# Splitting one 256-column product in five channel units of each FFN of a decoder trunk

## The chip, the core and the metric

The kernel runs on one core of a Trainium2 chip. The metric is the device time of one execution in microseconds, the median of several runs. The core's engines are TensorE (PE in the profile, with its weight loads shown apart as PEld), VectorE (DVE), ScalarE (ACT), GpSimd (POOL) and SyncE (SP), which issues most transfers.

## What is computed

Two decoder layers over a sequence of 256 tokens with 1024 channels, in fp32. Each layer is a SwiGLU FFN at half weight, a token mixer (a state-space branch and a gated delta-rule branch side by side), and a second FFN. Only the FFN matters here; there are four in all.

```python
def swiglu(x, w_in, w_out):
    gate, up = jnp.split(x @ w_in, 2, axis=-1)
    return (jax.nn.silu(gate) * up) @ w_out

for l in range(DEPTH):
    h = h + 0.5 * swiglu(rms_norm(h, ffn1_norm[l]), ffn1_w_in[l], ffn1_w_out[l])
    ...
    h = h + merged @ w_out[l]
    h = h + 0.5 * swiglu(rms_norm(h, ffn2_norm[l]), ffn2_w_in[l], ffn2_w_out[l])
return rms_norm(h, final_norm)
```

Here `w_in` has 1024 rows and 5632 columns (2816 gates and 2816 ups), and `w_out` 2816 rows and 1024 columns.

## The kernel before

**Precision.** Every large product is done in three matmuls. Each fp32 operand is kept as a rounded part (`whi`, `uTh`) and the remainder (`wlo`, `uTl`), both of a rounded fp32 type that TensorE takes in one pass. The helper `mm3w` (lines 300 to 303) multiplies rounded weights with rounded input, rounded weights with the input's remainder, and the weights' remainder with the rounded input, all into the same PSUM columns. In the profile these are lines L301, L302 and L303. `mm3` (L296 to L298) is the same with the activations as the stationary operand and 512 columns of weights moving.

**Weights.** All weights come through one stream of 512 KB pieces in DRAM. `load` starts a transfer into one of five `wraw` buffers (or a `wfirst` buffer for the first piece of a group), `prep` rounds it on ScalarE into one of five `whi` buffers (L67) and takes the remainder on VectorE into `wlo` (L70). `take` hands the next pair to the matmuls and keeps the preparation up to five pieces ahead. For some pieces VectorE also takes differences of raw weights (the `wfirst<-wraw,wfirst` and `wraw<-wraw` rows).

**One FFN.** The string `FFN` gives its order. First come 256 gate and up columns by tokens (`f`, tile `f`). Then follow 20 *channel units* (`c`, tile `fc`), each 128 gate and 128 up columns: `chan_chunk` takes two weight pieces and runs, for gate and for up (`a`), over eight blocks `kt` of 128 input channels, one `mm3w` each. This makes 48 matmuls of 256 columns (the 256 tokens), each with a weight load of 128 by 128. Behind a unit ScalarE takes the silu of the gate half (`sg`) and VectorE multiplies with the up half (`g2`). Four transposes (tile `gT`, L498) stand between the first and the second unit.

The output product `w_out` is done partly in blocks in which seven products of sums and differences stand for eight, as in Strassen's scheme (`block_sums` on the activations, differences in `prep` on the weights). Its first four products of each block pair are the *groups* (`A`, tile `p`, 24 matmuls of 512 columns each), and they stand between channel units: behind the first 8 units, then behind 4, 4 and 2 more. The last 2 units follow the fourth group. Then the *last stage* (`B` and `d`, tile `o`) does the remaining block products and the plain ones, while VectorE adds up the blocks in `join` (tiles `u`, `h`).

**Order.** The program text sets the order on TensorE. On the other engines a scheduler places the instructions by its own estimate of when each can run; the pools (five `whi`, five `wlo`, five `wraw`, four `acc` banks in PSUM) set when a buffer may be written again.

Of the kernel before, what the change touches and what calls it, by code (L numbers as in the profile page):

```python
# [16 lines left out]
P = 128  # L17
# [19 lines left out]
FFN = "f" + 8 * "c" + "A" + 4 * "c" + "A" + 4 * "c" + "A" + 2 * "c" + "A" + 2 * "c" + "BdBBBddddd"  # L37
# [15 lines left out]
def trunk_kernel(ctx, tc, x, wst, wsm, norms, lpar, rpar, cst, out):  # L53
    nc = tc.nc
    V, A, G, PE = nc.vector, nc.scalar, nc.gpsimd, nc.tensor
# [10 lines left out]
    def act(o, i, func=AF.Copy, **kw):  # L66
        return A.activation(out=o, in_=i, func=func, **kw)  # L67

    def tt(o, a, b, op):
        return V.tensor_tensor(out=o, in0=a, in1=b, op=op)  # L70
# [9 lines left out]
    def f(ap):  # L80
        return ap.bitcast(F32)

    def tmp2(name):
        return s2.tile([P, 512], F32, tag="s2", name=name)
# [97 lines left out]
    def take():  # L182
        j = state["taken"]
        state["taken"] = j + 1
        ahead("loaded", min(plan[min(j + NSPL, n_forms) - 1][2] + NRAW - 1, n_raw), load)
        ahead("prepped", min(j + 1 if state["hold"] else j + NSPL, n_forms), prep)
        return halves.pop(j)
# [109 lines left out]
        PE.matmul(ps, lh, rl, start=False, stop=False)  # L297
        return PE.matmul(ps, ll, rh, start=False, stop=stop)  # L298

    def mm3w(ps, wh, wl, mh, ml, start, stop):  # L300
        PE.matmul(ps, wh, mh, start=start, stop=False)  # L301
        PE.matmul(ps, wh, ml, start=False, stop=False)  # L302
        PE.matmul(ps, wl, mh, start=False, stop=stop)  # L303

    def tok_chunk(ps, ks):
# [13 lines left out]
                        kt == KT - 1,  # L319
                    )  # L320

    def chan_chunk(ps):

        ws = [take(), take()]
        for a in range(2):
            for q in range(2):
                wh, wl = ws[q]
                for k in range(4):
                    kt = 4 * q + k
                    c0 = k * 256 + a * P  # L330
                    mm3w(
                        ps[:, a * 256 : (a + 1) * 256],
                        wh[:, c0 : c0 + P],
                        wl[:, c0 : c0 + P],
                        uTh[:, kt, :],
                        uTl[:, kt, :],
                        kt == 0,
                        kt == KT - 1,
                    )

    def out_chunks(ps, stat, ks, last, group=1, split=False, first=None):
# [87 lines left out]
    def ffn(nxt):  # L429
        gh = [slots.tile([P, 8, S], F32R, tag=t_, name="gh") for t_ in ("sA", "sB", "sC")]  # L430
        gl = [slots.tile([P, 8, S], F32R, tag=t_, name="gl") for t_ in ("sD", "sE", "sF")]

        bsa = slots.tile([P, 2, 2, 3, P], F32R, tag="sG", name="bsa")
        bsb = slots.tile([P, 16, P], F32R, tag="sH", name="bsb")
        bsc = slots.tile([P, 4, 2, P], F32R, tag="sI", name="bsc")
        bsd = s2.tile([P, 2, 2, P], F32R, tag="s2", name="bsd")
        bsb3 = bsb[:, 0:12].rearrange("p (i o j) t -> p i o j t", i=2, o=2)
        bsb1 = bsb[:, 12:16].rearrange("p (i o) t -> p i o t", i=2)

        def sums(p, j):  # L440

            q, i = (p - 1) // 2, (p - 1) % 2
            if j < 3:
                b = (bsa[:], bsb3)[q % 2]
                return b[:, i, 0, j, :], b[:, i, 1, j, :]
            b = (bsc[:, 0:2], bsc[:, 2:4], bsb1, bsd[:])[q]
            return b[:, i, 0, :], b[:, i, 1, :]

        def block_sums(p, g2):

            sf = tmp2("sf")
            a11, a21, a12, a22 = (g2[:, j * P : (j + 1) * P] for j in range(4))
            s1, s2_, s3, s4 = (sf[:, j * P : (j + 1) * P] for j in range(4))
            tt(s1, a21, a22, ALU.add)
            tt(s3, a11, a21, ALU.subtract)
            tt(s2_, s1, a11, ALU.subtract)
            tt(s4, a12, s2_, ALU.subtract)
            q, i = (p - 1) // 2, (p - 1) % 2
            h3, l3 = ((bsa[:], bsb3)[q % 2][:, i, o] for o in range(2))
            h1, l1 = sums(p, 3)  # L460
            s3v = sf[:, 0 : 3 * P].rearrange("p (j t) -> p j t", j=3)
            act(h3, s3v)
            act(h1, s4)
            tt(l3, s3v, f(h3), ALU.subtract)
            tt(l1, s4, f(h1), ALU.subtract)

        def split(k0, bv):
            oh = gh[k0 // 8][:, k0 % 8 : k0 % 8 + 2, :]
            ol = gl[k0 // 8][:, k0 % 8 : k0 % 8 + 2, :]
            act(oh, bv)  # L470
            tt(ol, bv, f(oh), ALU.subtract)

        def stat(k, t):
            return (gh[k // 8][:, k % 8, t * P : (t + 1) * P], gl[k // 8][:, k % 8, t * P : (t + 1) * P])

        ps = [accb("f0"), accb("f1")]
        tok_chunk(ps, range(KT))
        gt = []
        for t in range(2):
            sg = tmp2("sg")  # L480
            act(sg[:, 0:256], ps[t][:, 0:256], AF.Silu)
            tt(sg[:, 256:512], sg[:, 0:256], ps[t][:, 256:512], ALU.mult)
            gt.append(sg[:, 256:512])
        todo, pb, n = FFN[1:], {}, 0
        for c in range(FC - 1):
            g2 = tmp2("g2")
            for a in range(2):
                ps = accb("fc")
                chan_chunk(ps)
                sg = s2.tile([P, S], F32, tag="ca", name="sg", bufs=2)  # L490
                act(sg[:], ps[:, 0:S], AF.Silu)
                tt(g2[:, a * S : (a + 1) * S], sg[:], ps[:, S : 2 * S], ALU.mult)
                todo = todo[1:]
                if c == 0 and a == 0:
                    bank = trb("gT")
                    for k in range(2):
                        for t in range(2):
                            PE.transpose(bank[:, k * S + t * P : k * S + (t + 1) * P], gt[t][:, k * P : (k + 1) * P], ident)  # L498
                    split(0, bank[:].rearrange("p (k t) -> p k t", k=2))
            split(2 * c + 2, g2[:].rearrange("p (k t) -> p k t", k=2))  # L500
            if c + 1 <= PAIRS[-1][-1]:
                block_sums(c + 1, g2)
            if todo[0] == "A":
                if not pb:
                    pb.update({i: trb(f"p{i}") for i in (1, 6, 5, 7)})
                four = [
                    (pb[1], lambda p: stat(2 * p, 0), PAIRS[n]),
                    (pb[5], lambda p: sums(p, 0), PAIRS[n]),
                    (pb[7], lambda p: sums(p, 2), PAIRS[n]),
                    (pb[6], lambda p: sums(p, 1), PAIRS[n]),  # L510
                ]
                block_products(four, n == 0, n == len(PAIRS) - 1)
                todo = todo[1:]
                n += 1
        po = [[accb("o"), accb("o")] for _ in range(2)]

        return close_blocks(po, stat, sums, pb, nxt)
# [841 lines left out]
```

## Time and profile before

| | us |
|---|---|
| median of three runs | 1576.33 |
| lowest and highest of them | 1573.42, 1577.17 |
| the profiled execution | 1574.73 |
| its span, first to last instruction | 1573.0 |
| first FFN, first channel unit to last stage | 25.12 to 160.25 |
| groups of output products in the first FFN, start | 70.60, 98.70, 126.75, 143.50 |
| channel units of the other FFNs, start | 618.05, 804.08, 1393.89 |

The granted TensorE clock of the profiled execution has a mean of 0.999 of full speed. A row of a group has the line, the engine, the operation, the output tile and the inputs, the shapes and the count; then the busy time, the mean length of one instruction, and the idle time before them. Matmuls are pipelined: a 256-column matmul is shown some 0.28 us long, while the next one starts 0.11 to 0.12 us later. How fast a stream runs is therefore read from start to start, not from lengths. A timeline row gives start and length in us, and in square brackets how long its engine had been idle and what ended that.

### The profile page before, as it was taken

The numbers are of one execution on the slowest core, as the hardware profiler recorded it, in microseconds if no ns is written. First come the engines' busy times: TensorE is split into PE (matmuls) and PEld (weight loads), VectorE is DVE, ScalarE is ACT, GpSimd is POOL, SyncE is SP. The second block draws the span as 40 slices with busy tenths as digits, with TensorE's granted clock in tenths as the row PEclk, the third lists the DMA queues.
The fourth block names the chain that finished last, engine by engine and source line by source line (L and its number), as shares of the span: only waits on it lengthen the run. The fifth ranks groups of instructions, "written<-read, shape, count | busy, mean of one in ns | idle before, by whom it ended". The sixth has DMA issues, their size and how long they took to land.

```text
span 1573.0 us, 28904 instructions
## 1 busy us (share of the span) xinstructions
PE 1544.0 (98%) x11432; PEld 1393.4 (89%) x11432; DVE 1254.2 (80%) x1888; ACT 950.7 (60%) x1534; POOL 53.8 (3%) x60
## 2 busy tenths in 40 slices
PE   8999999999999999999999999999999999999997
PEld 7999779999888888999789997899998888899995
DVE  6878868967899766878777888699589987677887
ACT  5656568766666645555555566776756665455554
POOL 0000010000000000000000001010000000000000
PEclk9999999999999999999999999999999999999999
DMA  8565565553565566565765456555345556555554
GB/s 297 199 201 186 185 213 188 168 164 114 180 212 164 183 205 192 169 207 181 243 206 191 166 186 223 192 188 188 115 137 200 175 185 215 176 191 187 161 186 133
DMA packets 94221, 293.12 MB, mean 186 GB/s; under 512 B 22325, under 2 KB 23301, under 8 KB 93062
## 3 DMA queue, kind: packets, MB, share of 16 engines
q1 hardware_dynamic: 94086, 291.29, 56.5%
q8 instruction: 89, 1.46, 0.4%
q14 instruction: 46, 0.38, 0.1%
HBM read 289.33 MB, written 1.92 MB: 185 GB/s over the span
## 4 chain that ended last, share of the span: by engine, by line
PE 68%; DVE 14%; DMA 7%; issue 5%; ACT 4%; POOL 1%; SPq 0%; POOLq 0%; ACTq 0%; DVEq 0%
PE fc L301 9%; PE fc L302 9%; PE fc L303 9%; DVE wlo L70 7%; DMA wraw<-in_wst_dram 4%; PE b L298 3%; PE t L297 3%; PE t L296 2%; PE t L298 2%; PE b L297 2%; PE b L296 2%; DVE ca L73 2%; ACT whi L67 2%; PE p L297 2%; PE p L298 2%
## 5 line engine op out<-in xcount | busy, mean ns | idle before, releaser
L70 DVE TENSOR_TENSOR wlo<-wraw,whi 128x1024 fp32r<-128x1024 f32 x488 | 592.3, 1222 | 176.8 <-ACT whi L67 172.3
L67 ACT ACTIVATE whi<-wraw 128x1024 fp32r<-128x1024 f32 x488 | 511.9, 1060 | 276.9 <-PE fc L302 96.0
L301 PE MATMUL fc<-uW,whi 128*128 128x256 f32 x1280 | 359.2, 281 | 0.0
L303 PE MATMUL fc<-uW,wlo 128*128 128x256 f32 x1280 | 358.9, 280 | 0.0
L302 PE MATMUL fc<-uW,whi 128*128 128x256 f32 x1280 | 358.9, 280 | 0.0
L303 PEld LDWEIGHTS fc<-uW,wlo 128*128 128x128 f32 x1280 | 243.6, 190 | 0.0
L301 PEld LDWEIGHTS fc<-uW,whi 128*128 128x128 f32 x1280 | 241.7, 189 | 0.8
L302 PEld LDWEIGHTS fc<-uW,whi 128*128 128x128 f32 x1280 | 240.3, 188 | 0.8
L67 ACT ACTIVATE whi<-wfirst 128x1024 fp32r<-128x1024 f32 x64 | 68.0, 1062 | 65.9 <-PE fc L302 50.9
L296 PE MATMUL t<-whi,uW 128*128 128x512 f32 x256 | 102.1, 400 | 0.0
L297 PE MATMUL t<-wlo,uW 128*128 128x512 f32 x256 | 100.6, 393 | 0.4 <-DVE wlo L70 0.4
L298 PE MATMUL t<-whi,uW 128*128 128x512 f32 x256 | 100.7, 393 | 0.0
L70 DVE TENSOR_TENSOR wlo<-wfirst,whi 128x1024 fp32r<-128x1024 f32 x64 | 78.3, 1223 | 8.8 <-ACT whi L67 8.8
L296 PE MATMUL b<-whi,bh 128*128 128x512 f32 x192 | 76.3, 399 | 0.3 <-ACT bh L67 0.2
L297 PE MATMUL b<-wlo,bh 128*128 128x512 f32 x192 | 74.9, 390 | 0.0
L298 PE MATMUL b<-whi,bl 128*128 128x512 f32 x192 | 74.3, 394 | 0.6 <-DVE bl L70 0.6
L70 DVE TENSOR_TENSOR wfirst<-wraw,wfirst 128x1024 f32<-128x1024 f32 x48 | 58.7, 1222 | 19.1 <-DMA wraw<-in_wst_dram 18.7
L301 PE MATMUL xs<-uW,whi 128*128 128x256 f32 x256 | 72.7, 284 | 0.0
L297 PE MATMUL o<-wlo,gh 128*128 128x512 f32 x160 | 64.5, 403 | 7.1 <-DVE wlo L70 6.9
L303 PE MATMUL xs<-uW,wlo 128*128 128x256 f32 x256 | 71.1, 278 | 0.0
L302 PE MATMUL xs<-uW,whi 128*128 128x256 f32 x256 | 71.0, 277 | 0.0
L296 PE MATMUL o<-whi,gh 128*128 128x512 f32 x160 | 62.1, 392 | 0.3 <-ACT whi L67 0.3
(315 smaller groups left out, 3385.8 us busy)
## 6 DMA issues: line engine op xcount, KB each, us to landing
wraw<-in_wst_dram SPq DMA_DIRECT2D x504, 512.0 KB, 4.5
wfirst<-in_wst_dram SPq DMA_DIRECT2D x16, 512.0 KB, 6.1
dc<-rdram SPq DMA_DIRECT2D x8, 1024.0 KB, 8.5
nw<-in_norms_dram SPq DMA_DIRECT2D x6, 512.0 KB, 5.9
gb<-rdram SPq DMA_DIRECT2D x8, 256.0 KB, 5.5
h<-in_x_dram SPq DMA_DIRECT2D x4, 256.0 KB, 5.9
out_dram<-fo SPq DMA_DIRECT2D x4, 256.0 KB, 2.0
dq<-X SPq DMA_DIRECT2D x2, 256.0 KB, 5.4
```

Of the source, the lines that this page charges most:

```text
L67: return A.activation(out=o, in_=i, func=func, **kw)
L70: return V.tensor_tensor(out=o, in0=a, in1=b, op=op)
L73: return V.scalar_tensor_tensor(out=o, in0=a, scalar=s, in1=b, op0=op0, op1=op1)
L296: PE.matmul(ps, lh, rh, start=start, stop=False)
L297: PE.matmul(ps, lh, rl, start=False, stop=False)
L298: return PE.matmul(ps, ll, rh, start=False, stop=stop)
L301: PE.matmul(ps, wh, mh, start=start, stop=False)
L302: PE.matmul(ps, wh, ml, start=False, stop=False)
L303: PE.matmul(ps, wl, mh, start=False, stop=stop)
```

## The change

In five channel units of each FFN, one of the 48 matmuls is replaced by two of 128 columns each: first and second half of the tokens, with the same weights, into the two halves of the same PSUM columns. It is the product of rounded weights and the input's remainder, at `a == 0` and `kt == 1`, so the fifth matmul of the unit. The five units are the third one (`c == 1`, `a == 0`) and the first one behind each of the four groups. What is computed stays the same.

```diff
-    def mm3w(ps, wh, wl, mh, ml, start, stop):
+    def mm3w(ps, wh, wl, mh, ml, start, stop, cut=False):
         PE.matmul(ps, wh, mh, start=start, stop=False)
-        PE.matmul(ps, wh, ml, start=False, stop=False)
+        if cut:
+            PE.matmul(ps[:, :P], wh, ml[:, :P], start=False, stop=False)
+            PE.matmul(ps[:, P:], wh, ml[:, P:], start=False, stop=False)
+        else:
+            PE.matmul(ps, wh, ml, start=False, stop=False)
         PE.matmul(ps, wl, mh, start=False, stop=stop)
...
-    def chan_chunk(ps):
+    def chan_chunk(ps, cut=False):
...
                         kt == 0,
                         kt == KT - 1,
+                        cut and a == 0 and kt == 1,
                     )
...
-        todo, pb, n = FFN[1:], {}, 0
+        todo, pb, n, cut = FFN[1:], {}, 0, False
...
-                chan_chunk(ps)
+                chan_chunk(ps, cut or (c, a) == (1, 0))
+                cut = False
...
-                todo = todo[1:]
+                todo, cut = todo[1:], True
                 n += 1
```

On TensorE, at the start of the third unit of the first FFN, the program had these rows (the number behind a tile's name tells buffers of one name apart; L301 to L303 are the three matmuls of one `mm3w`):

```order
L301 MATMUL fc_425<-uW_108,whi_281 128x256 [waits PE_49,Activation_49]
L302 MATMUL fc_425<-uW_108,whi_281 128x256
L303 MATMUL fc_425<-uW_108,wlo_282 128x256 [waits DVE_49]
L301 MATMUL fc_425<-uW_108,whi_281 128x256
L302 MATMUL fc_425<-uW_108,whi_281 128x256
L303 MATMUL fc_425<-uW_108,wlo_282 128x256
```

and now has these (line 303 and 304 are the halves, 306 and 307 the old second and third matmul):

```order
L301 MATMUL fc_425<-uW_108,whi_281 128x256 [waits PE_49,Activation_49]
L306 MATMUL fc_425<-uW_108,whi_281 128x256
L307 MATMUL fc_425<-uW_108,wlo_282 128x256 [waits DVE_49]
L301 MATMUL fc_425<-uW_108,whi_281 128x256
L303 MATMUL fc_425<-uW_108,whi_281 128x128
L304 MATMUL fc_425<-uW_108,whi_281 128x128
L307 MATMUL fc_425<-uW_108,wlo_282 128x256
```

One row has become two, and no wait has come or gone. The same stands behind each group, where the last rows of the group (tile `p6`) run straight into the unit:

```order
L297 MATMUL p6_847<-wlo_781,bsa_177 128x512 [waits DVE_49]
L298 MATMUL p6_847<-whi_780,bsa_177 128x512
L296 MATMUL p6_847<-whi_780,bsa_177 128x512
L297 MATMUL p6_847<-wlo_781,bsa_177 128x512
L298 MATMUL p6_847<-whi_780,bsa_177 128x512
L301 MATMUL fc_899<-uW_108,whi_852 128x256 [waits Activation_49]
L306 MATMUL fc_899<-uW_108,whi_852 128x256
L307 MATMUL fc_899<-uW_108,wlo_853 128x256 [waits DVE_49]
L301 MATMUL fc_899<-uW_108,whi_852 128x256
L303 MATMUL fc_899<-uW_108,whi_852 128x128
L304 MATMUL fc_899<-uW_108,whi_852 128x128
L307 MATMUL fc_899<-uW_108,wlo_853 128x256
```

Before, the row of line 303 and the row of line 304 were one row of line 302 there too. The scheduler, which sees two instructions more, has also moved a few rows on the other engines, the same ones in each FFN. On VectorE, around the preparation of the last group's weights, the order was

```order
L70 TENSOR_TENSOR wlo_1569<-wfirst_1507,whi_1568 128x1024 [waits PE_49,Activation_49]
L70 TENSOR_TENSOR g2_1555<-sg_1621,fc_1556 128x256 [waits Activation_49]
L70 TENSOR_TENSOR wfirst_1507<-wraw_1531,wfirst_1507 128x1024 [waits DVE_49]
L70 TENSOR_TENSOR wlo_1626<-wraw_1519,whi_1625 128x1024 [waits Activation_49]
L70 TENSOR_TENSOR wlo_1631<-wfirst_1507,whi_1630 128x1024 [waits PE_49,Activation_49]
```

and is now

```order
L70 TENSOR_TENSOR wlo_1572<-wfirst_1510,whi_1571 128x1024 [waits PE_49,Activation_49]
L70 TENSOR_TENSOR wlo_1630<-wraw_1522,whi_1629 128x1024 [waits PE_49,Activation_49]
L70 TENSOR_TENSOR g2_1558<-sg_1625,fc_1559 128x256 [waits Activation_49]
L70 TENSOR_TENSOR wfirst_1510<-wraw_1534,wfirst_1510 128x1024 [waits DVE_49]
L70 TENSOR_TENSOR wlo_1635<-wfirst_1510,whi_1634 128x1024 [waits PE_49,Activation_49]
```

The remainder of the group's third piece has gone ahead of a `g2`, and carries a wait for TensorE itself; on ScalarE the rounding of the same piece has gone ahead of the `sg` that `g2` reads. In the last stage VectorE had

```order
L70 TENSOR_TENSOR wlo_1970<-wraw_1871,whi_1969 128x1024 [waits Activation_49]
L70 TENSOR_TENSOR wlo_1980<-wfirst_1507,whi_1979 128x1024 [waits Activation_49]
L73 SCALAR_TENSOR_TENSOR u2_1961<-p7_848,u2_1961 128x512
L70 TENSOR_TENSOR wlo_1992<-wraw_1904,whi_1991 128x1024 [waits DMAHW1_49,Activation_49]
L70 TENSOR_TENSOR wlo_2004<-wraw_1906,whi_2003 128x1024 [waits DMAHW2_49,Activation_49]
```

and now has

```order
L70 TENSOR_TENSOR wlo_1975<-wraw_1876,whi_1974 128x1024 [waits Activation_49]
L73 SCALAR_TENSOR_TENSOR u2_1966<-p7_849,u2_1966 128x512
L70 TENSOR_TENSOR wlo_1985<-wfirst_1510,whi_1984 128x1024 [waits Activation_49]
L70 TENSOR_TENSOR wlo_1997<-wraw_1909,whi_1996 128x1024 [waits DMAHW1_49,Activation_49]
L70 TENSOR_TENSOR wlo_2009<-wraw_1911,whi_2008 128x1024 [waits DMAHW2_49,Activation_49]
```

An addition of `join` has gone ahead of one remainder. Two more remainders change places there with the row next to them, once with a `g2` and once with the next addition, and on SP one weight transfer changes places with its neighbour.

## The prediction

> **What bounds the kernel now.** I read the page first (busy shares, chain of waits, groups), then the stretches of the channel units (busy time, count and clock by window), then single rows of the timeline.
>
> ```profile
> PE 1544.0 (98%) x11432; PEld 1393.4 (89%) x11432; DVE 1254.2 (80%) x1888; ACT 950.7 (60%) x1534; POOL 53.8 (3%) x60
> PE 68%; DVE 14%; DMA 7%; issue 5%; ACT 4%; POOL 1%; SPq 0%; POOLq 0%; ACTq 0%; DVEq 0%
> L302 PE MATMUL fc<-uW,whi 128*128 128x256 f32 x1280 | 358.9, 280 | 0.0
> ACT whi L67 <- PE fc L302: 35.1, 29, 3.1
> ```
>
> TensorE holds 68% of the chain, and its `fc` matmuls (the channel units) wait for nothing: idle time before them is 0.0. The last row is from the waits of ScalarE between 25 and 165 us, most of the first FFN: the engine that prepares the weights waited 35.1 us for TensorE there. So a channel unit takes as long as its 48 matmuls take, and their pace is the price. That pace has two values. The next rows are windows restricted to the `fc` tile on PE (from:to, length, busy and count, granted clock, DMA share, GB/s); the windows from 37, 630, 815 and 1406 us are the same units of FFN one to four.
>
> ```profile
> 37.00:70.00 33.00, 33.00 (x282) 1.00 0.59 202
> 630.00:663.00 33.00, 33.00 (x283) 1.00 0.50 156
> 815.00:848.00 33.00, 33.00 (x294) 1.00 0.50 155
> 1406.00:1439.00 33.00, 33.00 (x282) 1.00 0.49 155
> 105.00:126.00 21.00, 21.00 (x181) 1.00 0.55 180
> ```
>
> The third FFN issues 294 matmuls in 33 us, the others 282 or 283. The clock is 1.00 in all, and the second and fourth have the third's DMA share, so neither clock nor transfers make the difference. Exact starts (start, length, engine and line) at both ends of six whole units:
>
> ```profile
> 36.68 0.28 PE L301 MATMUL fc<-uW,whi 128*128 128x256 f32 x1
> 70.60 0.39 PE L296 MATMUL p<-whi,gh 128*128 128x512 f32 x1
> 815.63 0.28 PE L301 MATMUL fc<-uW,whi 128*128 128x256 f32 x1
> 848.27 0.39 PE L296 MATMUL p<-whi,gh 128*128 128x512 f32 x1
> ```
>
> Slow pace: (70.60 - 36.68) / 288 = 117.8 ns a matmul. Quick pace: (848.27 - 815.63) / 288 = 113.3 ns. The difference, 4.44 ns, is 0.21 us a unit. The windows at 105 us and those like it behind the other groups (x181 in 21 us) show the slow pace in every unit behind a group of output products. What sets it? The handover rows:
>
> ```profile
> 75.86 0.39 PE L298 MATMUL p<-whi,bsa 128*128 128x512 f32 x1
> 76.09 0.28 PE L301 MATMUL fc<-uW,whi 128*128 128x256 f32 x1
> 30.59 0.60 PE L498 MATMUL gT<-cs,sg 128*128 128x128 f32 x4
> 30.95 0.36 PE L301 MATMUL fc<-uW,whi 128*128 128x256 f32 x1
> 31.15 0.28 PE L302 MATMUL fc<-uW,whi 128*128 128x256 f32 x1
> 31.27 0.28 PE L303 MATMUL fc<-uW,wlo 128*128 128x256 f32 x1
> 810.41 0.28 PE L303 MATMUL fc<-uW,wlo 128*128 128x256 f32 x1
> 810.53 0.28 PE L301 MATMUL fc<-uW,whi 128*128 128x256 f32 x1
> 811.10 0.28 PE L303 MATMUL fc<-uW,wlo 128*128 128x256 f32 x1
> ```
>
> The same four transposes stand before the second unit of each FFN: in the first FFN the stream behind them stays slow (31.27 - 31.15 = 0.12 us), in the third it settles at 0.114 us ((811.10 - 810.53) / 5). So the pace is a state of the stream: once entered it holds until something narrower or wider comes between, and the same code can land in either. Groups of 512-wide products always hand over into the slow one.
>
> **The change part by part.** Each cut replaces one 256-wide matmul, the fifth of its unit, by two of 128 columns with a weight load each. There are five a FFN, twenty in all.
>
> *Price of a cut.* The trace has no split of these products. The nearest rows are 128-wide matmuls with loads of their own:
>
> ```profile
> 381.16 1.05 PE L901 MATMUL vnb<-rh,TT 128*128 128x128 f32 x8
> 382.18 0.28 PE L302 MATMUL xs<-uW,whi 128*128 128x256 f32 x1
> L226 PE MATMUL nw<-row,one 1*128 1x512 f32 x4 | 3.7, 1085 | 2.3 <-DMA row<-in_norms_dram 2.3
> ```
>
> Between 381.16 and 382.18 lie eight narrow matmuls and one 256-wide: 1.02 / 9 = 0.113 us each; the transposes give (31.15 - 30.59) / 5 = 0.112. Two halves then cost 2 x 0.112 = 0.224 instead of 0.118: +0.106 us. From below: the columns are the same 256, so with the second load hidden the cut is free, 0; nothing in it can gain by itself. From above: the program issues two `nw` matmuls and the trace has four, so plain fp32 runs twice; if narrow halves ran like that, 4 x 0.112 - 0.118 = +0.33 us. I take 0.106, from the row with the same width and load. The Trainium skill (TensorE: Matmul & The Clock Gate, Back-to-back issue gap) gives about 81 ns for a load and a 128-wide matmul in a stream; by it the cut would cost an estimated 0.044 us, and the forecast be 1 us lower. The rows here, at 112 ns, disagree with it.
>
> *What a cut may bring.* It disturbs the locked stream: two narrow steps, then the 256-wide ones go on. If the stream relocks quick, every matmul behind it until the next group saves 4.44 ns. In the third unit 283 matmuls follow (6 x 48 - 5): 1.26 us. The first, second and fourth FFN are slow there: 3 x 1.26 = 3.77 us. The third is quick already; I take it to stay so, 0. Behind the groups stand 4, 4, 2 and 2 units, so 187, 187, 91 and 91 matmuls follow. The first three make 465 x 4.44 ns = 2.06 us a FFN, 8.26 us in all.
>
> *What the other engines make of it.* Preparation must follow. In the third FFN's quick stretch VectorE, the busier of the two, was busy 29.69 of 38 us:
>
> ```profile
> 810.00:848.00 38.00, 38.00 (x338) 38.00 (x336) 29.69 (x47) 20.97 (x31) 0.00 (x0) 1.00 0.53 166
> 142.22 1.06 ACT L67 ACTIVATE whi<-wfirst 128x1024 fp32r<-128x1024 f32 x1 [2.58 <-PE fc L302]
> 143.31 1.23 DVE L70 TENSOR_TENSOR wlo<-wfirst,whi 128x1024 fp32r<-128x1024 f32 x1 [1.05 <-ACT whi L67]
> 155.82 1.23 DVE L70 TENSOR_TENSOR wfirst<-wraw,wfirst 128x1024 f32<-128x1024 f32 x1 [3.24 <-DMA wraw<-in_wst_dram]
> 165.61 4.73 DMA wraw<-in_wst_dram
> 171.51 2.35 DVE wlo L70 x2
> ```
>
> Up to 143 us VectorE and ScalarE still wait for TensorE (1.05 and 2.58 us), so gains before that come through. From there VectorE's only long pause is for a transfer that its own work releases, and the chain through the last output stage (the last two rows, from the chain of waits) is VectorE and DMA. So I count nothing for the two units behind the fourth group, at 149 to 160 us: they could give 91 x 4.44 ns = 0.40 us less a cut, 0.30 us a FFN, 1.2 us in all. The fourth cut behind a group hides in the same way.
>
> *The moved rows.* ScalarE takes one weight rounding ahead of a `sg`, VectorE the remainder of it ahead of `g2`: same work, same release, and the product that comes later is not read before the last stage. In the last stage VectorE takes an addition of `join` ahead of a remainder:
>
> ```profile
> 176.65 1.22 DVE L70 TENSOR_TENSOR wlo<-wfirst,whi 128x1024 fp32r<-128x1024 f32 x1
> 177.79 0.69 DVE L73 SCALAR_TENSOR_TENSOR u<-p,u 128x512 f32<-128x512 f32 x1
> 178.39 1.22 DVE L70 TENSOR_TENSOR wlo<-wraw,whi 128x1024 fp32r<-128x1024 f32 x1
> 178.51 0.39 PE L297 MATMUL o<-wlo,gh 128*128 128x512 f32 x1
> ```
>
> That remainder, needed at 178.51, would end 0.60 us (178.39 - 177.79) later, at 178.47 instead of 177.87: just in time, so 0; without that cover up to 0.6 us a FFN. The two other swaps there have more room. One weight transfer changes places with its neighbour on SP, free as long as ScalarE's wait for TensorE lasts.
>
> *Sum.* 3.77 + 8.26 = 12.03 us gained; 4 cuts x 4 FFNs x 0.106 = 1.70 us paid: 10.3 us net. The profiled execution took 1574.73 us with a span of 1573.0; so span 1562.7, that execution 1564.4, and on the median of the three runs 1576.33 - 10.3 = 1566.0 us. A measurement here tells about 0.3%, 4.7 us, from no change.
>
> **Rivals.**
>
> 1. *The cut does not change the pace.* For: the transposes, narrow too, left three FFNs of four slow. Against: the third FFN, which left it behind the same rows, and the first unit of the first FFN, which starts slow and turns quick by itself:
>
> ```profile
> 25.36 0.28 PE L303 MATMUL fc<-uW,wlo 128*128 128x256 f32 x1
> 25.47 0.28 PE L301 MATMUL fc<-uW,whi 128*128 128x256 f32 x1
> 29.91 0.28 PE L301 MATMUL fc<-uW,whi 128*128 128x256 f32 x1
> 30.25 0.28 PE L301 MATMUL fc<-uW,whi 128*128 128x256 f32 x1
> ```
>
> (three steps from 29.91 to 30.25 are 113 ns each). Then only the cuts remain: 16 to 20 x 0.106 = 1.7 to 2.1 us, 1578.2. The Trainium skill (same page and section) knows one gap a width, 256 / 2.4 + 2.5 = 109 ns, and no second pace; by that rule a cut could only cost. The two paces of the trace disagree with it.
>
> 2. *It changes at some places.* Only behind the groups: 8.26 - 1.70 = 6.6 us, 1569.8. Only in the third units: 3.77 - 1.70 = 2.1, 1574.3. Or at all of them with dear halves: 12.03 - 16 x 0.33 = 6.8, 1569.6. For it: the two kinds of place come from different streams, transposes and 512-wide products.
>
> 3. *Dear halves with no change of pace, slower.* Place: the two narrow matmuls of each cut. At 0.33 us each, 16 to 20 of them cost 5.3 to 6.6 us: 1582. It decides from 4.7 / 16 = 0.29 us a cut. For: no narrow product of these rounded operands stands in the trace. Against: narrow matmuls run at 0.112 us a pass.
>
> **How the numbers follow.** Forecast 0.47, rival 1 0.20, rival 2 0.20 (0.13 of it over 4.7 us of gain, 0.07 within), rival 3 0.13. Faster 0.47 + 0.13 = 0.60, same 0.20 + 0.07 = 0.27, slower 0.13. The forecast's own range is 1563 to 1569. The low end of the whole: 1566.0 less 1.2 (fourth groups count) less 1.7 (free cuts) less some 1.5 for seven units of the mixer that could relock quick (0.21 each): 1561.5. The high end stops between rivals 1 and 3, at 1580.
>
> **What would show it.** Right: windows at 37, 630 and 1406 us with some 294 `fc` matmuls in 33 us, those behind the groups with about 185 in 21; 0.22 us across the halves; the output stage about 2 us earlier a FFN with no more idle time before its `o` matmuls. Wrong: 282 and 181 again (rival 1); a mix (rival 2); 0.45 us across the halves (rival 3); a quick third FFN turned slow by its cut, which costs 1.26 us; `o` matmuls that wait for VectorE by as much as the units gained.

## The result, and the profile after

| kernel | us, median | lowest to highest | runs |
|---|---|---|---|
| before | 1576.59 | 1573.42 to 1577.17 | 4 |
| changed | 1568.47 | 1566.61 to 1569.1 | 4 |

The ratio is 0.9954, with a 95% interval of 0.9939 to 0.9969 (it is taken over the runs; the quotient of the two medians is 0.9949). By the medians the change takes 8.1 us off, where 10.3 us were forecast. The profiled execution took 1568.61 us with a span of 1566.8, against 1573.0 before, a difference of 6.2 us. In two later sets of runs, each beside the kernel before on one chip, the same kernel gave 1567.93 and 1567.06 us (ratios 0.9965, 0.9952 to 0.9977, and 0.9955, 0.9943 to 0.9967), so 6 to 8 us is the size of it.

The page of the changed kernel, the rows that answer to those shown of before:

```profile
PE 1535.5 (98%) x11452; PEld 1382.9 (88%) x11452; DVE 1252.7 (80%) x1888; ACT 949.7 (61%) x1534; POOL 53.7 (3%) x60
PE 67%; DVE 16%; DMA 6%; issue 5%; ACT 4%; POOL 1%; SPq 1%; POOLq 0%; ACTq 0%; DVEq 0%
L306 PE MATMUL fc<-uW,whi 128*128 128x256 f32 x1260 | 348.1, 276 | 0.0
L297 PE MATMUL o<-wlo,gh 128*128 128x512 f32 x160 | 65.4, 409 | 9.8 <-DVE wlo L70 9.6
```

TensorE still carries the chain, with twenty matmuls more (11452 against 11432) and 8.5 us less busy time; VectorE's share of the chain rose from 14 to 16%. The last row is the price side. On the page of before it reads:

```profile
L297 PE MATMUL o<-wlo,gh 128*128 128x512 f32 x160 | 64.5, 403 | 7.1 <-DVE wlo L70 6.9
```

So the output stages of the changed kernel wait 2.7 us longer for VectorE's remainders (9.6 against 6.9 us, all four FFNs).

The pace is read from windows on the `fc` tile (from:to, length, busy and count, granted clock, DMA share, GB/s). Of the changed kernel, the first behind the third unit's cut and the other two behind the first two groups of the first FFN:

```profile
37.50:68.50 31.00, 31.00 (x276) 1.00 0.62 206
80.00:95.00 15.00, 15.00 (x134) 1.00 0.44 149
108.00:122.00 14.00, 14.00 (x126) 1.00 0.45 152
```

Before, the same window behind the first group:

```profile
80.00:95.00 15.00, 15.00 (x130) 1.00 0.53 178
```

At 113.3 ns a window of 15 us holds 132 starts and at 117.8 ns 127, with up to three more that were under way at its edges; the counts of 134 and 130 are the quick and the slow pace, at the same granted clock. (The windows of 33 us that the prediction named cannot be filled: the 283 matmuls behind the third unit's cut take 32.1 us at the quick pace.) From start to start every one of the twenty cuts has the quick pace behind it; in three of the four third units the stream had been quick ahead of the cut as well. One cut row by row, the first behind a group:

```profile
74.35 0.39 PE L298 MATMUL p<-whi,bsa 128*128 128x512 f32 x1
74.58 0.28 PE L301 MATMUL fc<-uW,whi 128*128 128x256 f32 x1
74.70 0.28 PE L306 MATMUL fc<-uW,whi 128*128 128x256 f32 x1
74.81 0.28 PE L307 MATMUL fc<-uW,wlo 128*128 128x256 f32 x1
74.93 0.28 PE L301 MATMUL fc<-uW,whi 128*128 128x256 f32 x1
75.05 0.22 PE L303 MATMUL fc<-uW,whi 128*128 128x128 f32 x1
75.11 0.28 PE L304 MATMUL fc<-uW,whi 128*128 128x128 f32 x1
75.22 0.33 PE L307 MATMUL fc<-uW,wlo 128*128 128x256 f32 x1
75.39 0.28 PE L301 MATMUL fc<-uW,whi 128*128 128x256 f32 x1
75.51 0.29 PE L306 MATMUL fc<-uW,whi 128*128 128x256 f32 x1
...
75.98 0.28 PE L307 MATMUL fc<-uW,wlo 128*128 128x256 f32 x1
76.09 0.28 PE L301 MATMUL fc<-uW,whi 128*128 128x256 f32 x1
```

The stream arrives at 117 to 118 ns. The first half is over in 0.06 us (75.05 to 75.11), the second takes 0.11, and the matmul behind them 0.17 (75.22 to 75.39). From the first half to 75.39 is 0.345 us by the trace's nanoseconds, where two slow matmuls take 0.236: the cut costs 0.109 us. The weight loads (PEld) in this place start at 75.05, 75.17, 75.28 and 75.40 us, so they stand 0.11 us apart, further than the 0.06 us that the first half took. A few steps later the stream stands at 0.113 and stays there.

Where the time went, by stage. The *channel stage* of an FFN runs from the start of the first `fc` matmul to the start of the first `o` matmul, and the *last stage* from there to the start of the next part's first product (`t` or `f`; for the fourth FFN to the last matmul's end). In the first FFN these two starts are 25.12 and 160.25 us before and 25.00 and 156.83 us after; the second edge of the changed kernel:

```profile
156.72 0.28 PE L307 MATMUL fc<-uW,wlo 128*128 128x256 f32 x1
156.83 0.39 PE L296 MATMUL o<-whi,bsc 128*128 128x512 f32 x1
```

| us | FFN 1 | FFN 2 | FFN 3 | FFN 4 | sum |
|---|---|---|---|---|---|
| channel stage, before | 135.13 | 135.12 | 133.81 | 135.12 | 539.2 |
| channel stage, changed | 131.84 | 131.84 | 131.85 | 132.04 | 527.6 |
| last stage, before | 36.33 | 37.91 | 35.72 | 43.90 | 153.9 |
| last stage, changed | 36.91 | 39.13 | 36.93 | 44.70 | 157.7 |

The channel stages give 11.6 us and the last stages take 3.8 back; the two mixers together, each from its first `t` matmul to the first matmul of its output product, are 1.9 us longer (769.4 against 767.5), and what stands ahead of the channel stage of the first FFN is 0.1 us shorter. The experiments ask which cuts carry the 11.6, what makes the stream quick, and whether the 3.8 belongs to the change.

### The profile page after: what moved, and what is told of

The parts are those of the page before. It is cut to its first block, busy times and chain, and to the rows that moved or that the text cites. A ratio compares the mean times of both kernels' runs of the same rounds, so it can differ in the third digit from the quotient of the medians.

```text
span 1566.8 us, 28951 instructions
## 1 busy us (share of the span) xinstructions
PE 1535.5 (98%) x11452; PEld 1382.9 (88%) x11452; DVE 1252.7 (80%) x1888; ACT 949.7 (61%) x1534; POOL 53.7 (3%) x60
## 4 chain that ended last, share of the span: by engine, by line
PE 67%; DVE 16%; DMA 6%; issue 5%; ACT 4%; POOL 1%; SPq 1%; POOLq 0%; ACTq 0%; DVEq 0%
PE fc L301 7%; PE fc L307 7%; DVE wlo L70 7%; PE fc L306 7%; DMA wraw<-in_wst_dram 5%; PE t L297 3%; PE t L296 3%; PE t L298 3%; PE b L298 3%; PE b L297 2%; PE b L296 2%; ACT whi L67 2%; DVE ca L73 1%; PE xs L301 1%; PE xs L306 1%
## 5 line engine op out<-in xcount | busy, mean ns | idle before, releaser
L307 PE MATMUL fc<-uW,wlo 128*128 128x256 f32 x1280 | 354.7, 277 | 0.0
L301 PE MATMUL fc<-uW,whi 128*128 128x256 f32 x1280 | 354.0, 277 | 0.0
L306 PE MATMUL fc<-uW,whi 128*128 128x256 f32 x1260 | 348.1, 276 | 0.0
L301 PEld LDWEIGHTS fc<-uW,whi 128*128 128x128 f32 x1280 | 240.4, 188 | 0.8
L307 PEld LDWEIGHTS fc<-uW,wlo 128*128 128x128 f32 x1280 | 240.4, 188 | 0.0
L306 PEld LDWEIGHTS fc<-uW,whi 128*128 128x128 f32 x1260 | 236.5, 188 | 0.8
L301 PE MATMUL xs<-uW,whi 128*128 128x256 f32 x256 | 73.0, 285 | 0.0
L298 PE MATMUL o<-whi,gl 128*128 128x512 f32 x160 | 62.6, 391 | 0.0
```

## The experiments

Each ratio is that of the kernel to the kernel before in the same set of runs, with its 95% interval. In the first set the kernel before had a median of 1574.0 us (35 runs, 1570.04 to 1579.44), in the second 1574.02 (16 runs), in the third 1574.23 (17 runs). Each expectation was written ahead of its run and says itself what the theories named in it hold.

### Which cuts carry the gain

**Cuts behind the groups alone, and in the third unit alone.** Against the changed kernel:

```diff
-                chan_chunk(ps, cut or (c, a) == (1, 0))
+                chan_chunk(ps, cut)
```

```diff
-                chan_chunk(ps, cut or (c, a) == (1, 0))
+                chan_chunk(ps, (c, a) == (1, 0))
```

> Cuts behind the groups alone, rows moved on VectorE and ScalarE as by the change. Pace theory: all units behind groups at 113.3 ns, 2.06 + 0.40 us less a FFN less four cuts of 0.109 us, 8.1 us in the channel units; of that the last stage gives back about 0.9 us a FFN, as under the change, so 4 to 6 us faster on the span. Rival (the third unit's cut carries the gain): under 2 us.

> Cuts in the third units alone, the order of all other engines as before. Pace theory: 1.26 us less in each FFN whose first stretch is slow, less 0.109 a cut; with three slow FFNs 3.3 us faster, with one slow FFN (in the profile of the change the second unit was quick ahead of the cut in three of four) 0.8 us faster. Units behind the groups stay at 117.8 ns. Rival (cuts do nothing here): 0.4 us slower.

Groups alone: 1569.3 us, ratio 0.9961 (0.9949 to 0.9972). Third unit alone: 1574.05 us, 1.0 (0.9988 to 1.0012). The groups' cuts carry the whole gain that can be measured, and the third unit's cut none that shows. In the profiled execution with the groups' cuts alone the channel stages are 131.72, 131.71, 131.72 and 131.90 us, no longer than with all five: the units from the second to the eighth ran quick in all four FFNs without a cut. In the one with the third unit's cut alone three of the four were quick before that cut came.

**The change again.** No edit; the question is whether the pace behind the transposes belongs to the place or to the execution.

> The change itself, unaltered, beside runs of the kernel before on the same chip. Theory that the units behind the transposes fall into either pace anew in each execution: the units behind groups quick in all 16 stretches as in the first profile, the second unit quick in some FFNs and slow in others, the ratio near 0.995 to 0.996. Rival (the places are fixed by the code): the second unit quick in FFN one to three and slow in the fourth, again.

1567.93 us, 0.9965 (0.9952 to 0.9977). Behind the transposes the second unit was slow in the second FFN and quick in the others; in the changed kernel's first profile it was slow in the fourth alone, and in the profile of before in the first, second and fourth. The rows are the second matmul of the second unit and the first half of the cut, 51 matmuls later, in FFN two and three:

```profile
623.54 0.28 PE L306 MATMUL fc<-uW,whi 128*128 128x256 f32 x1
629.55 0.22 PE L303 MATMUL fc<-uW,whi 128*128 128x128 f32 x1
...
807.24 0.28 PE L306 MATMUL fc<-uW,whi 128*128 128x256 f32 x1
813.03 0.22 PE L303 MATMUL fc<-uW,whi 128*128 128x128 f32 x1
```

(629.55 - 623.54) / 51 = 117.8 ns, and (813.03 - 807.24) / 51 = 113.5 ns, by the same instructions. The slow one had settled, and the cut turned it: behind the cut the second FFN has the quick pace, 274 matmuls in 31 us.

```profile
631.00:662.00 31.00, 31.00 (x274) 1.00 0.54 165
```

The same happened in the other three profiles with one slow second unit and a cut in the third (the changed kernel's first, the third unit alone, and the one without the fourth cut). In the thirteen profiled executions that leave the second unit whole there are 52 such stretches; nine began slow, three of them in the profile that the prediction was made from. Elsewhere it is 6 of 48. It is not pure chance within an execution: where the first unit of an FFN ran slow, 17 cases, the second was quick each time; all nine slow ones are among the 35 cases with a quick first unit.

**No cut behind the fourth group.**

```diff
-                todo, cut = todo[1:], True
+                todo, cut = todo[1:], n < 3
```

> The change without the cut behind the fourth group. Theory (VectorE and DMA set the last stage from about 143 us of the first FFN): the channel units take 0.29 us longer a FFN, the last stage that much less, same median as the change within 0.3 us. Rival (the chain still runs through TensorE there): 4 x 0.29 = 1.2 us slower than the change.

1567.47 us, 0.996 (0.9944 to 0.9976), the same as the change. The two units behind the fourth group are slow again and the channel stages 132.12 to 132.31 us, 0.3 to 0.5 longer than the change's in three FFNs and 0.1 in the fourth; the last stages are shorter (36.48, 38.03, 36.69 and 43.02 us, 0.2 to 1.7 less than in the change's first profile; their sum, 154.2, is below that of each of the change's three profiles, 156.3 to 157.7). So in the traces what the fourth cut gains is handed back behind it; the medians agree, but could not tell the rival's 1.2 us.

**A cut in every unit.**

```diff
-                chan_chunk(ps, cut or (c, a) == (1, 0))
+                chan_chunk(ps, True)
```

> A cut in every one of the 20 units of each FFN, sixty more than the change. Price theory: 0.109 us each, 60 x 0.109 = 6.5 us slower than the change (5.9 if those behind the fourth group are hidden by VectorE), so 1 to 2 us faster than before. Rival with free halves: as the change, 8 us faster. Rival with halves at 0.33 us: 20 us slower than the change. The pace between two cuts should be 113.3 ns after about five matmuls.

1577.99 us, 1.0017 (1.0004 to 1.0031), by the medians 4 us slower than before where the expectation had 1 to 2 us faster: 60 further cuts use up the gain and more. The channel stages are 133.93 us each, 2.0 longer than the change's for fifteen more cuts, 0.14 us a cut (0.2 of the 2.0 is a slow unit, below). That brings their sum to 535.7 us, only as much as the 535.4 of a later variant that takes the time of before (the split earlier in the group). So most of what it takes above the kernel before lies outside the channel stages; VectorE's order is changed at more places here than by the change, and no run tells what these cost. In the rows, the first halves of the cuts of three successive units:

```profile
31.66 0.22 PE L303 MATMUL fc<-uW,whi 128*128 128x128 f32 x1
...
37.42 0.22 PE L303 MATMUL fc<-uW,whi 128*128 128x128 f32 x1
...
42.99 0.22 PE L303 MATMUL fc<-uW,whi 128*128 128x128 f32 x1
```

A unit with a cut that runs quick takes 42.99 - 37.42 = 5.57 us, 0.13 above 48 x 0.1133 = 5.44. So inside a quick stream a cut costs a little more than the 0.109 us it costs a slow one, which would have paid 4.44 ns a step anyway. The unit between the first two takes 5.76 us: it ran slow. Its cut came at the fifth matmul behind the transposes, before the stream had settled, and left it in the slow pace until the next cut, in all four FFNs. Without a cut in it that unit was slow in 9 of 52 cases, so a cut can also turn a stream the wrong way.

**The cut at the end of each stretch.** The same number of cuts, but in the last unit of each stretch, ahead of each group and of the last stage (`late`): the price without the gain.

```diff
-                        cut and a == 0 and kt == 1,
+                        cut and a == 1 and kt == 6,
...
-                chan_chunk(ps, cut or (c, a) == (1, 0))
+                chan_chunk(ps, todo[1] != "c")
```

> The same twenty cuts, each moved to the last unit ahead of a group (or of the last stage), seven matmuls from its end, so that hardly any matmul is left behind it. Pace theory: nothing left to save, only the price of 16 to 20 cuts at 0.109 us: 1.7 to 2.2 us slower than the kernel before, windows behind the groups still with 181 matmuls in 21 us. Rival (the gain comes from the moved rows or from anything else that two more instructions a unit bring): about 8 us faster, as the change was.

1578.34 us, 1.0022 (1.001 to 1.0034), 4.3 us slower than before. Every stretch behind a group ran slow, so it is the place of the cut and not its presence that brings the gain. The 4.3 us are more than its twenty cuts' 2.2 to 2.6 us (0.109 to 0.13 each); the rest stays unexplained (VectorE's rows are moved here too, other ones than by the change), and the interval, from 1.6 to 5.4 us, allows it to be nothing.

### What makes the stream quick

**The last product of a group in two halves of 256.** My reading so far was that the narrow halves are what shakes the stream loose, since weight loads 0.11 us apart do not hide behind a step of 0.06 us. This variant has no narrow matmul: it is the kernel before with the last 512-wide matmul of each group split.

```diff
-    def mm3(ps, lh, ll, rh, rl, start, stop):
+    def mm3(ps, lh, ll, rh, rl, start, stop, half=False):
         PE.matmul(ps, lh, rh, start=start, stop=False)
         PE.matmul(ps, lh, rl, start=False, stop=False)
+        if half:
+            PE.matmul(ps[:, 0:256], ll, rh[:, 0:256], start=False, stop=False)
+            return PE.matmul(ps[:, 256:512], ll, rh[:, 256:512], start=False, stop=stop)
         return PE.matmul(ps, ll, rh, start=False, stop=stop)
...
-                mm3(bank[:], sh, sl, wh[:, c], wl[:, c], begin and i == 0, end and i == 1)
+                mm3(bank[:], sh, sl, wh[:, c], wl[:, c], begin and i == 0, end and i == 1, half and i == 1 and bank is todo[-1][0])
```

> No narrow halves: units as before, and the last 512-column matmul of each group done as two of 256 columns. Theory that the stream relocks only behind a step in which loads, 0.11 us each, are slower than the columns they serve: 256 columns take about as long as a load, so the units behind the groups stay at 117.8 ns (181 in 21 us), time as before within 0.5 us. Rival (any break of the 512-column stream will do): 113.3 ns behind all groups at no price, 2.5 us a FFN less in the channel units, 8 us or more faster than before.

The expectation missed. 1566.06 us, 0.9953 (0.9937 to 0.997): as fast as the change, and all sixteen stretches behind the groups quick. The hand-over in this kernel:

```profile
74.32 0.39 PE L297 MATMUL p<-wlo,bsa 128*128 128x512 f32 x1
74.55 0.28 PE L299 MATMUL p<-whi,bsa 128*128 128x256 f32 x1
74.66 0.28 PE L300 MATMUL p<-whi,bsa 128*128 128x256 f32 x1
74.78 0.29 PE L304 MATMUL fc<-uW,whi 128*128 128x256 f32 x1
74.90 0.28 PE L305 MATMUL fc<-uW,whi 128*128 128x256 f32 x1
75.02 0.28 PE L306 MATMUL fc<-uW,wlo 128*128 128x256 f32 x1
75.14 0.28 PE L304 MATMUL fc<-uW,whi 128*128 128x256 f32 x1
75.25 0.28 PE L305 MATMUL fc<-uW,whi 128*128 128x256 f32 x1
75.36 0.28 PE L306 MATMUL fc<-uW,wlo 128*128 128x256 f32 x1
```

The two halves take 0.11 and 0.12 us, together what the whole took (0.23, 74.32 to 74.55), so this split is free; the first three `fc` steps take 0.12, and from there the stream is quick. The channel stages are 131.21, 131.39, 132.70 and 131.39 us (in the third FFN the second unit fell slow), elsewhere 0.4 to 0.7 below the change's. The theory that only a step bound by its loads relocks the stream falls. VectorE, ScalarE and SP run in the same order here as in the kernel before, so the gain does not hang on moved rows either.

**The same split, earlier in the group.** If any 256-wide matmul inside the group did it, the first of its four products would serve as well as the last. The edit is that of the variant before, with the first product in place of the last:

```diff
+                mm3(..., half and i == 1 and bank is todo[0][0])
```

> The kernel before with the last 512-wide matmul of the FIRST of the four products in each group done as two of 256; nine 512-wide matmuls follow before the channel unit, and the units are untouched. Theory B (what decides is the hand-over: a settled 512-wide stream at 226.7 ns that runs straight into the 256-wide one leaves it in the slow pace): by the ninth matmul behind it the 512-wide stream is settled again, all 16 stretches behind the groups start in the slow pace (187 matmuls at 117.8 ns), channel stages of 133.7 to 135.1 us as before, and the median stays within 0.3% of the kernel before, 1572 to 1576. Rival C (any 256-wide matmul inside the group turns the stream quick until something else comes between): quick stretches as in the variant with the last matmul split, channel stages near 131.4, 6 to 8 us faster.

1574.33 us, 1.0002 (0.9992 to 1.0012): the time of before. Eighteen 512-wide matmuls follow the split (not nine, as the expectation has it), and within six of them the group is back at 0.23 us a step. All sixteen stretches are slow. Hand-over and window behind the first group:

```profile
74.36 0.39 PE L301 MATMUL p<-whi,bsa 128*128 128x512 f32 x1
74.59 0.28 PE L304 MATMUL fc<-uW,whi 128*128 128x256 f32 x1
74.71 0.28 PE L305 MATMUL fc<-uW,whi 128*128 128x256 f32 x1
```

```profile
80.00:95.00 15.00, 15.00 (x130) 1.00 0.43 143
```

So behind the groups what decides is the last step ahead of the 256-wide stream, or the first ones in it. There this holds in every case seen: straight out of the 512-wide products the stream locked slow in all 64 stretches of four kernels (before, third unit alone, late, early) and behind the four uncut groups of the variant without the fourth cut; with a cut in the first unit, or with the last product split, it was quick in all.

**The split at the token-side units too.** The first unit of each FFN and the mixer's `t` units end in 512-wide matmuls as well.

```diff
                         kt == KT - 1,
+                        t == 1 and kt == ks[-1],
```

> The variant with the last 512-wide matmul of each group split in two of 256, and besides the last 512-wide matmul of every token-side unit split the same way (in the FFNs' first unit and the mixer's t units). Theory B: every 256-wide stream that starts straight behind a 512-wide one now starts quick: the first 48 fc matmuls of each FFN and the vv, zd and bc stretch behind the t units (up to 7 units of 48 matmuls a layer at 4.44 ns, 1.5 us a layer). In the trace that shows as 113.3 ns there in both layers. In the median at most 3 us less than the variant without it; as the cut at the vv unit moved the median by nothing that could be told, 0 to 3 us less is what I look for. Rival (the t units' stream is another: it settles at 228.8 ns and not at 226.7, and its hand-over follows another rule): the stretches keep the slow pace in some layers, no change in the median.

1565.4 us, 0.9939 (0.9928 to 0.9951), the lowest median of all; its interval overlaps those of the change and of the variant with the split at the groups alone, so it is not shown to be better than these, only than the kernel before. The first units of the FFNs were quick in three cases of four, which is no news: without a split or a cut they were quick in 32 of 48. The mechanism failed in the mixer: the stretch of `vv`, `zd` and `bc` units ran slow in both layers. Hand-over in the second layer:

```profile
1083.49 0.40 PE L297 MATMUL t<-wlo,uW 128*128 128x512 f32 x1
1083.72 0.28 PE L299 MATMUL t<-whi,uW 128*128 128x256 f32 x1
1083.84 0.28 PE L300 MATMUL t<-whi,uW 128*128 128x256 f32 x1
1083.96 0.28 PE L304 MATMUL vv<-uW,whi 128*128 128x256 f32 x1
...
1084.31 0.28 PE L304 MATMUL vv<-uW,whi 128*128 128x256 f32 x1
```

(1084.31 - 1083.96) / 3 = 0.117. Here the halves take 0.12 and 0.12, where at the groups they take 0.11 and 0.12. The `t` stream itself settles at 228.8 ns from start to start, the groups at 226.7. Behind the `t` stream both paces also occur without a split: in the twelve profiles that leave this stretch alone it was slow in 16 cases of 24. So the rule "512-wide products straight into a 256-wide stream lock it slow" holds for the groups alone. That the two 512-wide paces decide what follows them, and what a split does, fits, but was not tested.

**A cut in the mixer.** The change, and a cut at the `vv` unit that opens that stretch (`chan_chunk(ps, hp == 2)` there).

> The change and one more cut in the mixer of each layer, in the third of the units with tile vv, behind 24 matmuls of 512 columns; 307 matmuls of 256 columns follow without a break. In six profiles of these kernels that stretch was slow in 9 of 12 cases. Pace theory: quick in both layers, 307 x 4.44 = 1.36 us less where it would have been slow, less 0.12 us, so on average 0.9 us a layer and 1.8 us faster than the change; ratio to before near 0.994. Rival (later waits in the mixer take it back): as the change.

1568.24 us, 0.9964 (0.9952 to 0.9976). The four units from there on were quick in both layers of its profile, where the change's three profiles have them slow in both, but the median is that of the change, and the 1.8 us expected did not show. Inconclusive: the stretch that the cut turned is about four units and not the 307 matmuls of the expectation, and 4 x 0.21 = 0.85 us a layer is less than what these runs can tell.

**Change and split side by side.** Both once more in one set.

> The change itself once more, beside the variant with the wide split. All 16 stretches behind the groups quick; the second unit quick or slow by draw, each FFN for itself; median 1567 to 1569 where the kernel before stands at 1574 to 1576.

> The same kernel as the variant with the last 512-wide matmul of each group split, again, beside the change in one call. If the narrow halves' price of 0.11 us counts and the third unit's cut is worth about 0.2 us a FFN, the two differ by less than 2 us: 16 x 0.11 = 1.8 us to the good of this one, of which the fourth group's 0.4 is hidden, less some 0.8 for the third unit: about 0.5 us less than the change, not to be told apart. All 16 stretches behind the groups quick.

The change 1567.06 us, 0.9955 (0.9943 to 0.9967); the split 1567.63 us, 0.9955 (0.9943 to 0.9968). No difference that can be told. The split's channel stages are 131.20 to 131.21 us, the change's 131.84 to 132.03, 2.9 us over the four FFNs; its last stages are 1.5 us longer (157.8 against 156.3). The rest of these two profiles differs in parts that both kernels have alike: with the split the mixers are 2.8 us shorter and what stands ahead of the first FFN's channel stage 2.4 us longer. So the two differ by less than what an execution varies by.

### The last stages

The variant with the split runs VectorE, ScalarE and SP in the same order as the kernel before, the change does not. The wait rows of the first FFN's last stage (150 to 200 us: engine, line, releaser, us in all, times, longest), of before, of the change and of the split:

```profile
PE o L297 <- DVE wlo L70: 1.2, 3, 0.8
```

```profile
PE o L297 <- DVE wlo L70: 1.4, 3, 0.8
```

```profile
PE o L297 <- DVE wlo L70: 1.4, 3, 0.8
```

Both quick kernels wait 0.2 us longer, with the moved rows and without; both have a last stage of 36.9 us. So the moved rows cost nothing that shows. The row of waits alone does not tie the 0.6 us to TensorE's earlier arrival, for the variant with the split too early in the group, slow behind every group, also shows 1.4. The lengths do: the first FFN's last stage took 36.2 to 36.5 us in the five profiles that are slow behind the fourth group (before, third, late, early, and the one without the fourth cut), and 36.7 to 37.6 us in the nine that are quick there. VectorE moves with the channel stage only up to the fourth group. Of the changed kernel:

```profile
140.70 1.23 DVE L70 TENSOR_TENSOR wlo<-wfirst,whi 128x1024 fp32r<-128x1024 f32 x1 [1.21 <-ACT whi L67]
152.87 1.23 DVE L70 TENSOR_TENSOR wfirst<-wraw,wfirst 128x1024 f32<-128x1024 f32 x1 [3.19 <-DMA wraw<-in_wst_dram]
```

Before, these stood at 143.31 and 155.82: 2.6 and 2.95 us later, while TensorE's last stage came 3.42 us later (160.25 against 156.83). The difference of 0.5 us is about what the last stage is longer by.

The rest of the 3.8 us is put down to the spread between executions. The sum of the four last stages in the four profiles with slow groups is 153.9 (before), 155.1 (early), 156.0 (late) and 158.8 (third), a mean of 156.0; in the three profiles of the change it is 157.7, 157.2 and 156.3, a mean of 157.0. By these means about 1 us of it goes with the change, an estimate from seven profiles that spread by 5 us, and the profile of before stood at the favourable end. In the same way the mixers sum to 767.5 to 770.3 us in the one set and 769.4 to 772.2 in the other (767.3 to 772.8 in the other kernels with quick groups), by the same program; whether a part of that goes with the change was not settled.

## Why the prediction came close, point by point

1. *Two paces that lock.* Right. 113.3 and 117.8 ns are the only settled paces of `fc` in all fourteen profiles; the granted clock is 1.00 in every window shown.
2. *A cut in a slow stream makes it quick.* Right wherever the stream was slow: behind the sixteen groups, and in the one third unit of four that the first profile of the change had slow. So rival 1 fell. Rival 2's case of the groups alone (1569.8 us forecast) fell as a mechanism and holds as an account: the variant with those cuts alone took 1569.3 us, since the third units had little to give (point 5). The reason I leaned on, that narrow steps disturb a locked stream, is too special: a free step of another kind at the hand-over does the same.
3. *Price of a cut, 0.106 us.* Measured 0.109 us in a slow stream and 0.13 us in a quick one. The size is right, but not by two equal steps of 0.112 us: the halves take 0.06 and 0.11 us, and the matmul behind them 0.17. Rival 3's 0.33 us did not occur. The estimate of 0.044 us from the 81 ns a narrow matmul of the Trainium skill (TensorE: Matmul & The Clock Gate, Back-to-back issue gap) is not what these rows show: in the pair, one step takes 61 ns and the other 113.
4. *Behind the groups, 8.26 us, and 1.2 us behind the fourth not counted.* Right. By the terms the sixteen cuts should shorten the channel stages by 8.26 + 1.6 (the fourth groups', 4 x 0.40) - 16 x 0.109 = 8.1 us; the variant with these cuts alone stands 8.3 us below the one with the split too early in the group (527.1 against 535.4), both with quick second units in every FFN. In the variant without the fourth cut the last stages are shorter by what its channel stages are longer, and more, so the fourth group's share is handed back; its median, the same as the change's, agrees but could not show it alone.
5. *Third units, 3 x 1.26 = 3.77 us.* This term was mis-sized. In the execution that was profiled the 1.26 us were there to be had in three FFNs. The changed kernel's profile is shorter there, but by luck: in the first and the second FFN the unit ahead of the cut was quick by itself, and only in the fourth did the cut turn a slow stream. The prediction took the state behind the transposes, seen once in four places, for a property of the place ("the first, second and fourth FFN are slow there"). It is drawn anew in each execution, and slow in 6 of 48 cases outside that profile. So the term is worth about 4 x 1.26 x 6/48 = 0.6 us, and the four cuts cost 4 x 0.13 = 0.5. The prediction had set the mixed state down as an argument for rival 1 and did not draw this conclusion from it.
6. *VectorE sets the end of the last stage, the moved rows cost nothing.* Right in kind. "No more idle time before its `o` matmuls" was wrong: they wait 2.7 us longer in all, since VectorE follows TensorE only as far as its own work and transfers allow; about 1 us shows in the last stages' lengths on the mean.
7. *The sum.* 8.1 us from the cuts behind the groups, the fourth among them, 0.1 from the third units, less about 1 in the last stages: 7.2 us, where the three sets of runs measured 8.1, 6.1 and 7.2. The mixers are left out of this sum, since whether their 2 us or so go with the change is open. The forecast of 10.3 was too high by most of the third units' term. It came out as close as it did in part by luck: the forecast reached from 1563 to 1569 us, the first set's 8.1 us is the largest of the three, and the 6.1 us of the second, taken off the 1576.33 us that the forecast started from, would have given 1570.2.

Left open: why a 256-wide stream that runs straight out of the groups' products locks slow, why the `t` units' products do not obey the same split, and what the mixer's paces are worth.

## What to carry to other kernels

Read the pace of a long matmul stream from start to start, stretch by stretch: if the same shape runs at two paces at the same clock, look at what stands ahead of each stretch, and try to change that step at no cost (split the last wide matmul) before paying for an extra one inside the stream, and look in the trace whether it took: behind the groups it did, behind the `t` units it did not. Before a state seen in one execution is priced, look whether the same code shows it in each repetition of the loop; where it differs there, price it by its share and not by the one draw. An engine that runs close behind the bottleneck hands back what is gained in the last stretch ahead of it, so count only the gains from which it can still follow.

## What the runs showed of the hardware that I had not expected

- A 256-wide stream, each matmul with its own weight load, settles at 113.3 or at 117.8 ns and stays there over 187 matmuls and more. The last step ahead of it can decide: 512-wide products at 226.7 ns led into the slow pace in 64 of 64 stretches, and with the last of them split in two halves of 256 columns into the quick one in 48 of 48. Products of the same width at 228.8 ns led into either: the FFNs' first units were quick in 32 of 48 cases, the mixer's `vv` stretch in 8 of 24.
- The same transposes lead into the one or the other from execution to execution: 9 of 52 slow. None of the nine followed a slow first unit.
- A 128-wide pair with a load for each half delays the stream by 0.06 + 0.11 + 0.17 us instead of two steps: the delay falls on the matmul behind the second half as well, while the loads there start 0.11 to 0.12 us apart. The 512-wide product split in halves of 256, both with the same weights, costs nothing (0.11 + 0.12 against 0.23 us).
